# A two-layer hybrid attention backbone: SBUF-only elementwise work of the attention phases moved from VectorE and ScalarE to GpSimd

## Chip, cores and metric

The kernel runs on one core of one Trainium2 chip, in one launch. The metric is the device time in microseconds. The engines are called by their short names: PE (TensorE), DVE (VectorE), ACT (ScalarE), POOL (GpSimd) and SP (SyncE, which here only issues DMAs).

## What is computed

Two layers of a flow-matching backbone work on 512 latent tokens and 256 context tokens of width 1024, in fp32. Each layer, cut to what matters:

```python
hx = rms_norm(x, p['norm1_g']) * (1 + sc1x) + sh1x      # adaLN modulation from SiLU(c); ctx likewise
(lw_q, ..., ln_v) = split_in(hx @ p['w_in'])            # one projection to 3072 columns
out_w = window_attention(q, k, v, k_c, v_c, p['a_sink'])           # group A: windowed, rotary, sink
out_f = rms_norm(diff_attention(q, k, v, k_c, v_c, lam)) * ...     # group B: P0 - lam * P1, rotary
out_r = rms_norm(o_f + flip(o_b), p['c_gn_g']) * gate              # group C: retention, no softmax
out_n = neighbourhood_attention(q, k, v, k_c, v_c, p['d_rpb'])     # group D: 2-D neighbourhood, bias
x = x + g1x * (concat(out_w, out_f, out_r, out_n) @ p['w_out'])
x = x + g2x * (square(relu(h2 @ p['w_mlp1'])) @ p['w_mlp2'])
```

The context stream goes the same way in the first layer; the output is the latent stream.

## The kernel before

**Precision by halves.** Every large product is made of three matmuls. An fp32 value is split into a rounded part `hi` (type fp32r) and a remainder `lo = src - hi`; the product is hi\*hi + hi\*lo + lo\*hi. `split` (L274 to L276) does this: ACT copies `src` to `hi` with rounding (L275), DVE subtracts (L276).

```python
def split(src, hi, lo):
    S.activation(hi, src, AF.Copy)
    V.tensor_tensor(lo, src, hi.bitcast(F32), op=OP.subtract)
```

It is used for weights (`wload`, L278: tiles `wh` and `wl`, 128x512, four buffers of each), for transposed probabilities (`pth`, `ptl`, from PSUM), for C's decayed scores (L963 to L965: `P` is in SBUF, again `pth` and `ptl`), for B's stacked queries and keys (`sp`, in `stack32`, L617) and for the attention outputs ahead of the output projection (`oh`, `ol`, in `out_ac`, L1033). `kstack` (L603) does the same by hand for the keys of A, C and D (`ks`, `kl`, L610), 64 partitions at a time, and SP copies each part to the other 64 partitions.

**Stages.** A layer has an attention phase and an MLP phase. In the attention phase seven units stand in the order a0 b0 b1 c0 c1 d0 d1. Each has an input part (`in_a` to `in_d`: input projection, norms, rotary embedding, stacking) and an attention part (`at_a` to `at_d`: scores, probabilities, transposition, product with V). `weave` (L106) runs a unit's attention part and fills in the input parts of later units and then the output projection (`out_ac`), by planned costs and leads, so that PE has gemm work between the steps of an attention chain. The framework's scheduler then turns the program into one fixed order of instructions per engine, with priorities: a weight's split gets a bonus of 40 (`WPRI`). Each engine works off its own order and stops at an instruction whose input isn't there.

**The chains in the attention parts.** A and D (`band_pair`, L726) take two score tiles at a time: row maximum on DVE, exponential with row sum on ACT (L752), reciprocal on DVE, normalisation of each tile on ACT (L759), transposition on PE. B (`at_b`, L832) needs no normalisation of that kind: DVE combines two exponentials (L860). C multiplies scores by a decay table on DVE (L962), splits the result and goes straight to the product with V, where `pvmm` (L699) issues matmuls with `pth` (L703) and `ptl` (L702, L705). The decay tables `tb` and `tx` of a head come from `ctables` (L895): loads, exponentials, and two sums of 128x512 on DVE (L915). The rotary embedding (L651 to L656): ACT scales, DVE shuffles, multiplies by the cosine table (L654), multiplies the shuffled copy by the sine table, adds.

`PTS` = 5 buffers are shared by `pth`, `ptl` and the copies of outputs; `htile` tiles (16) hold first the normalised input of the phase and then, buffer by buffer as the last input tile no longer needs them, `oh` and `ol`.

## Time and profile before

| | us |
|---|---|
| median of 3 runs | 1896.78 (1894.79 to 1897.86) |
| profiled execution, its own time | 1897.64 |
| span of the profile | 1895.6 |
| PE busy in the span | 1843.1 (97%) |
| DVE busy | 1307.4 (69%) |
| ACT busy | 973.4 (51%) |
| POOL busy | 0.2 (4 instructions) |

The span is what the hardware profiler recorded on the core; the execution's own time has 2.0 us around it. Attention of layer 0 lies at about 100 to 520 us, the MLP of layer 0 to about 1120, attention of layer 1 at 1130 to 1560, its MLP after that. A busy PE isn't PE at its peak: matmuls overlap, and a matmul's recorded length is longer than its distance to the next. The chain that ended last, followed back from the end, lies on PE for 89% of the span.

### The profile page before, as it was taken

To read this page: it belongs to the slowest core of one execution; us is meant where nothing else is said; L and a number is where in the kernel's file an instruction comes from. 1 tells how busy PE (TensorE), PEld (TensorE's weight loads), DVE (VectorE), ACT (ScalarE), POOL (GpSimd) and SP (SyncE) were. 2 spreads that over 40 slices of the span, in tenths; PEclk is the share of its full clock that TensorE was granted. 3 is DMA by queue.
4 is the path that set the end of the run, shared out by engine and by line. 5 is a ranking of instruction groups with operands and counts; after the bars stand their busy time and mean duration, and the time that the engine had idled before them with its cause. 6 is when DMAs were issued, how large, how long until landed. Compare 5 with 4: busy or idle time off the path is not lost.

```text
span 1895.6 us, 29665 instructions
## 1 busy us (share of the span) xinstructions
PE 1843.1 (97%) x10899; PEld 1519.8 (80%) x10899; DVE 1307.4 (69%) x3005; ACT 973.4 (51%) x1934; POOL 0.2 (0%) x4
## 2 busy tenths in 40 slices
PE   7998889999999999999999999999899999999999
PEld 3786667778878888888888777878677788989897
DVE  5788867788777847847847367898788764545453
ACT  4677656668654214223323356877577763334242
POOL 0000000000000000000000000000000000000000
PEclk8999989999999999999999999999899999999999
DMA  8324334432323523423422352332243223232322
GB/s 297 99 79 122 100 120 131 148 95 65 109 95 106 157 93 117 151 95 117 150 95 89 111 172 83 83 96 79 85 133 95 75 95 100 90 100 90 100 90 95
DMA packets 110417, 208.68 MB, mean 110 GB/s; under 512 B 14272, under 2 KB 20160, under 8 KB 110272
## 3 DMA queue, kind: packets, MB, share of 16 engines
q1 hardware_dynamic: 110272, 206.78, 34.7%
q8 instruction: 86, 1.41, 0.3%
q14 instruction: 59, 0.48, 0.1%
HBM read 182.09 MB, written 5.24 MB: 99 GB/s over the span
## 4 chain that ended last, share of the span: by engine, by line
PE 89%; ACT 5%; DVE 3%; DMA 2%; issue 1%; SPq 0%; ACTq 0%; DVEq 0%
PE mm L315 23%; PE mm L317 23%; PE mm L316 23%; PE ps L697 3%; PE po L703 2%; PE po L705 2%; PE ps L262 1%; PE ps L850 1%; PE pt L241 1%; ACT pth L275 1%; PE pt L257 1%; PE pt L869 1%; PE pt L798 1%; ACT P L856 1%; DMA zm<-in_dd_dram 1%
## 5 line engine op out<-in xcount | busy, mean ns | idle before, releaser
L275 ACT ACTIVATE wh<-wr 128x512 fp32r<-128x512 f32 (+1 forms) x414 | 252.9, 614 | 645.3 <-PE mm L316 605.0
L317 PE MATMUL mm<-hh,wl 128*128 128x512 f32 (+2 forms) x1680 | 548.8, 327 | 6.7 <-DVE wl L276 6.6
L315 PE MATMUL mm<-hh,wh 128*128 128x512 f32 (+2 forms) x1680 | 551.2, 328 | 3.0 <-ACT zq L651 1.7
L316 PE MATMUL mm<-hl,wh 128*128 128x512 f32 (+2 forms) x1680 | 549.8, 327 | 0.0
L276 DVE TENSOR_TENSOR wl<-wr,wh 128x512 fp32r<-128x512 f32 (+1 forms) x414 | 275.4, 667 | 162.4 <-ACT wh L275 156.4
L315 PEld LDWEIGHTS mm<-hh,wh 128*128 128x128 f32 x1680 | 318.3, 190 | 39.9 <-issue 7.6
L317 PEld LDWEIGHTS mm<-hh,wl 128*128 128x128 f32 x1680 | 318.9, 190 | 34.7 <-DVE wl L276 7.7
L316 PEld LDWEIGHTS mm<-hl,wh 128*128 128x128 f32 x1680 | 318.0, 189 | 28.1 <-issue 3.5
L316 PE MATMUL mm<-ml,wh 128*128 128x512 f32 (+1 forms) x768 | 273.2, 356 | 0.0
L315 PE MATMUL mm<-mh,wh 128*128 128x512 f32 (+1 forms) x768 | 272.7, 356 | 0.0
L317 PE MATMUL mm<-mh,wl 128*128 128x512 f32 (+1 forms) x768 | 272.4, 355 | 0.0
L316 PEld LDWEIGHTS mm<-ml,wh 128*128 128x128 f32 x768 | 145.2, 189 | 24.5 <-issue 4.5
L315 PEld LDWEIGHTS mm<-mh,wh 128*128 128x128 f32 x768 | 145.2, 189 | 21.9 <-issue 0.4
L317 PEld LDWEIGHTS mm<-mh,wl 128*128 128x128 f32 x768 | 145.1, 189 | 21.2 <-issue 1.2
L394 DVE SCALAR_TENSOR_TENSOR acc<-wm,silp,acc 128x512 f32<-128x512 f32 x196 | 138.9, 747 | 21.9 <-DMA wm<-in_wmod_dram 21.7
L1127 DVE SCALAR_TENSOR_TENSOR x<-mm,modc,x 128x512 f32<-128x512 f32 (+1 forms) x96 | 63.4, 660 | 116.6 <-PE mm L317 116.6
L703 PE MATMUL po<-pth,vv 128*128 128x256 f32 (+2 forms) x328 | 105.5, 328 | 8.9 <-ACT pth L275 8.1
L276 DVE TENSOR_TENSOR ptl<-pt,pth 128x512 fp32r<-128x512 f32 (+3 forms) x148 | 92.4, 630 | 27.9 <-ACT pth L275 26.4
L275 ACT ACTIVATE pth<-pt 128x512 fp32r<-128x512 f32 (+3 forms) x148 | 80.2, 547 | 32.2 <-PE pt L869 21.6
L1111 DVE TENSOR_TENSOR zq<-mm,nacc 128x256 f32<-128x256 f32 (+1 forms) x128 | 61.9, 484 | 44.5 <-PE mm L317 43.0
L703 PEld LDWEIGHTS po<-pth,vv 128*128 128x128 f32 x328 | 61.8, 189 | 32.3 <-ACT pth L275 24.0
L705 PE MATMUL po<-ptl,vv 128*64 128x256 f32 (+2 forms) x256 | 78.3, 318 | 2.9 <-DVE ptl L276 2.3
(251 smaller groups left out, 2701.3 us busy)
## 6 DMA issues: line engine op xcount, KB each, us to landing
wr<-in_w_dram SPq DMA_DIRECT2D x272, 256.0 KB, 2.6
wm<-in_wmod_dram SPq DMA_DIRECT2D x112, 256.0 KB, 2.8
wr<-in_win_dram SPq DMA_DIRECT2D x96, 256.0 KB, 3.0
wr<-in_wmodh_dram SPq DMA_DIRECT2D x48, 256.0 KB, 3.3
st<-sp SPq DMA_DIRECT2D x96, 96.0 KB, 2.2
w<-in_wmod_dram SPq DMA_DIRECT2D x16, 384.0 KB, 7.1
tx<-in_dd_dram SPq DMA_DIRECT2D x8, 512.0 KB, 4.4
zm<-in_dd_dram SPq DMA_DIRECT2D x16, 256.0 KB, 3.5
```

What stands on the lines that cost most here:

```text
L241: T.matmul(pj, lhsT=gmean[w], rhs=sq[:, 256 * j:256 * j + 256], start=True, stop=add is None)
L275: S.activation(hi, src, AF.Copy)
L276: V.tensor_tensor(lo, src, hi.bitcast(F32), op=OP.subtract)
L315: T.matmul(p, lhsT=wh, rhs=ah[:, s:s + l], start=(k == 0), stop=False)
L316: T.matmul(p, lhsT=wh, rhs=al[:, s:s + l], start=False, stop=False)
L317: T.matmul(p, lhsT=wl, rhs=ah[:, s:s + l], start=False, stop=(k == len(act) - 1))
L394: V.scalar_tensor_tensor(acc[:, v], r, sil[:, k, v:v + 1], acc[:, v], op0=OP.mult, op1=OP.add)
L697: T.matmul(o, lhsT=x, rhs=y, start=(i == 0), stop=(i == 1))
L703: T.matmul(po[:, c0:c0 + l], lhsT=vv[:, hh, t], rhs=ph, start=start, stop=stop)
L705: T.matmul(po[0:64, c0:c0 + l], lhsT=vv[:, hh, t, 0:64], rhs=pl, start=False, stop=False)
L1111: V.tensor_tensor(r[:, s:s + l], p[:, :l], y2[:, s:s + l], op=OP.mult)
L1127: V.scalar_tensor_tensor(xx, p, modc[:, 40 + m, s // 512:s // 512 + 1], xx, op0=OP.mult, op1=OP.add)
```

## The change

In the attention phases these operations go from DVE to POOL, unchanged in shape and operands: the remainders of weights (128 instructions), of C's scores (56), of the keys of A, C and D (20), of B's stacked queries and keys (8), and of the attention outputs of groups A, B and C (12), the product with the cosine table in the rotary embedding (14), and the sums of C's decay tables (16). The normalisation of the probabilities of A and D (80) goes from ACT to POOL, as a product with a per-row scalar. The remainders of transposed probabilities stay on DVE, since these read PSUM, and in the MLP phases (`wrest[0] = V` behind the attention phase) the weights' remainders stay there too. Priorities, buffers and `weave`'s costs are the same. Behind the first two added lines, numbers of lines in the changed kernel are 2 to 4 higher (L915 becomes L918, L705 L708).

```diff
--- before.py
+++ after.py
@@ -154,7 +154,7 @@
 @with_exitstack
 def body(ctx: ExitStack, tc, A):
     nc = tc.nc
-    V, S, G, T, SY = nc.vector, nc.scalar, nc.gpsimd, nc.tensor, nc.sync
+    V, S, PL, T, SY = nc.vector, nc.scalar, nc.gpsimd, nc.tensor, nc.sync
 
     cons = ctx.enter_context(tc.tile_pool(name="cons", bufs=1))
     main = ctx.enter_context(tc.tile_pool(name="main", bufs=1))
@@ -271,9 +271,11 @@
             V.scalar_tensor_tensor(sq[:, s:s + l], ap, EPS if eps else 0.0, sq[:, s:s + l], op0=OP.add, op1=OP.mult)
         V.scalar_tensor_tensor(sq[:, :n], sq[:, :n], -3.0, e3[:, :n], op0=OP.add, op1=OP.mult)
 
-    def split(src, hi, lo):
+    def split(src, hi, lo, eng=V):
         S.activation(hi, src, AF.Copy)
-        V.tensor_tensor(lo, src, hi.bitcast(F32), op=OP.subtract)
+        eng.tensor_tensor(lo, src, hi.bitcast(F32), op=OP.subtract)
+
+    wrest = [PL]
 
     def wload(src, k0=0, k1=8, dst=None):
 
@@ -288,7 +290,7 @@
                 hi = wp.tile([128, 512], F32R, name=nm("wh"), tag="wh", bufs=WB)
                 lo = wp.tile([128, 512], F32R, name=nm("wl"), tag="wl", bufs=WB)
             with tc.high_priority(offset=WPRI):
-                split(r, hi[:, :128 * n], lo[:, :128 * n])
+                split(r, hi[:, :128 * n], lo[:, :128 * n], wrest[0])
             res += [(hi[:, 128 * k:128 * k + 128], lo[:, 128 * k:128 * k + 128]) for k in range(n)]
         return res
 
@@ -467,6 +469,7 @@
         rb = rowb[:, L, :]
         modc = modcs[L]
 
+        wrest[0] = PL
 
         att = ExitStack()
         ap_ = att.enter_context(tc.tile_pool(name=f"att{L}", bufs=1))
@@ -607,7 +610,7 @@
                 a, b = HALF[h], HALF[1 - h]
                 S.activation(x[a, :n], t[a, :n], AF.Copy)
                 KCOPY(x[b, :n], x[a, :n])
-                V.tensor_tensor(y[a, :n], t[a, :n], x[a, :n].bitcast(F32), op=OP.subtract)
+                PL.tensor_tensor(y[a, :n], t[a, :n], x[a, :n].bitcast(F32), op=OP.subtract)
                 KCOPY(y[b, :n], y[a, :n])
             return st, lo
 
@@ -617,7 +620,7 @@
         def stack32(t, n, order):
 
             parts = [main.tile([128, 768], F32R, name=nm("sp"), tag="zq", bufs=ZQ)[:, :n] for _ in range(2)]
-            split(t[:, :n], *parts)
+            split(t[:, :n], *parts, PL)
             st = [u3r("st") for _ in range(4)]
             for i, x in enumerate(st):
                 for r, w in enumerate(order):
@@ -651,7 +654,7 @@
                     S.activation(t[:, 0:512], p, AF.Copy, scale=gc)
                     sh = zq()
                     V.stream_shuffle(sh[:, 0:512], t[:, 0:512], mask)
-                    V.tensor_tensor(t[:, 0:512], t[:, 0:512], tab[:, 0], op=OP.mult)
+                    PL.tensor_tensor(t[:, 0:512], t[:, 0:512], tab[:, 0], op=OP.mult)
                     V.tensor_tensor(sh[:, 0:512], sh[:, 0:512], tab[:, 1], op=OP.mult)
                     V.tensor_tensor(t[:, 0:512], t[:, 0:512], sh[:, 0:512], op=OP.add)
                 elif permute and s == 0:
@@ -756,7 +759,7 @@
                 V.tensor_tensor(sm[:, 6:8], sm[:, 6:8], sm[:, 10:12], op=OP.add)
             V.reciprocal(sm[:, 12:14], sm[:, 6:8])
             for i, (P, _, w) in enumerate(res):
-                S.activation(P[:, :w + 256], P[:, :w + 256], AF.Copy, scale=sm[:, 12 + i:13 + i])
+                PL.tensor_scalar(P[:, :w + 256], P[:, :w + 256], sm[:, 12 + i:13 + i], None, op0=OP.mult)
             yield 0
             return [(P, kts) for P, kts, _ in res]
 
@@ -912,7 +915,7 @@
                 SY.dma_start(out=tw[:, 0:512], in_=A['dd'][:, 1920 + 512 * t:2432 + 512 * t])
                 S.activation(tw[:, 0:512], tw[:, 0:512], AF.Exp, scale=nlb)
                 S.activation(tx[:, t], tx[:, t], AF.Exp, scale=lf)
-                V.tensor_tensor(tx[:, t], tx[:, t], tw[:, 0:512], op=OP.add)
+                PL.tensor_tensor(tx[:, t], tx[:, t], tw[:, 0:512], op=OP.add)
             return tb, tx
 
         def in_c(u):
@@ -961,7 +964,7 @@
                         P = ptile()
                         V.tensor_tensor(P[:, :l], p[:, :l], dk, op=OP.mult)
                         pth, ptl = ptt()
-                        split(P[:, :l], pth[:, :l], ptl[:, :l])
+                        split(P[:, :l], pth[:, :l], ptl[:, :l], PL)
                         pvmm(po, 0, l, vv, hh, t, pth[:, :l], ptl[:, :l], i == 0, i == len(kts) - 1)
                         yield 3 * l * .43
                     ev = evac_t(po, l)
@@ -1035,7 +1038,7 @@
             osp = []
             for c in range(6):
                 hi, lo = htile("oh"), htile("ol")
-                split(of[c][:, :nq], hi[:, :nq], lo[:, :nq])
+                split(of[c][:, :nq], hi[:, :nq], lo[:, :nq], PL)
                 osp.append((hi, lo))
             for m in range(8):
                 xr = u3("xr")
@@ -1055,6 +1058,7 @@
         cost_at = {x: c * 1e3 for x, c in zip('abcd', [[CA0, CB0, CC0, CD0], [CA1, CB1, CC1, CD1]][L])}
         weave(units, ins, ats, cost_in, cost_at, out_ac(), [[L0_0, L0_1, L0_2, L0_3, L0_4, L0_5, L0_6, L0_7], [L1_0, L1_1, L1_2, L1_3, L1_4, L1_5, L1_6, L1_7]][L], lambda: tc.high_priority(offset=BOOST))
         att.close()
+        wrest[0] = V
 
 
         mlp = ExitStack()
```

The scheduler orders all engines anew. Three places:

The first is on DVE before, in layer 1, at the end of c0's input part (`zq`, `gt` are C's gate, `zm` and `gp` its tables, `sm` and `P` belong to B); `wl` is the remainder of a weight tile.

```order
L933 SCALAR_TENSOR_TENSOR zq_14184<-zq_14184,zq_14187 128x512
L903 TENSOR_SCALAR zm_14198<-gp_14194,lg_11949 128x128
L934 SCALAR_TENSOR_TENSOR gt_14183<-gt_14183,gsc_11929,zq_14184 128x512
L904 TENSOR_SCALAR gp_14194<-gp_14194,nlg_11983 128x128
L276 TENSOR_TENSOR wl_14427<-wr_14424,wh_14426 128x512
L905 TENSOR_TENSOR gp_14194<-gp_14194,zm_14198 128x128
L724 ISA P_14292,sm_14291<-ps_14294,zcol 128x256
```

In the changed kernel the same tile stands on POOL behind other weight tiles:

```order
L276 TENSOR_TENSOR wl_14233<-wr_14230,wh_14232 128x512
L276 TENSOR_TENSOR wl_14239<-wr_14236,wh_14238 128x512
L276 TENSOR_TENSOR wl_14421<-wr_14418,wh_14420 128x512
L276 TENSOR_TENSOR wl_14427<-wr_14424,wh_14426 128x512
L918 TENSOR_TENSOR tx_14195<-tx_14195,zm_14206 128x512
L918 TENSOR_TENSOR tx_14195<-tx_14195,zm_14211 128x512
```

`wl_14427` no longer stands behind the gate and the tables; behind it on POOL come the two sums of a table.

The second is C in layer 0, first head, six score tiles of 512 columns. On DVE before, from the second tile's remainder (`P` is the decayed score, `tx` the next head's table):

```order
L276 TENSOR_TENSOR ptl_3797<-P_3794,pth_3796 128x512
L962 TENSOR_TENSOR P_3915<-ps_3906,gp_3383 128x512
L276 TENSOR_TENSOR ptl_3836<-P_3833,pth_3835 128x512
L962 TENSOR_TENSOR P_3938<-ps_3929,gp_3383 128x512
L276 TENSOR_TENSOR ptl_3895<-P_3892,pth_3894 128x512
L915 TENSOR_TENSOR tx_3734<-tx_3734,zm_3745 128x512
L915 TENSOR_TENSOR tx_3734<-tx_3734,zm_3750 128x512
L276 TENSOR_TENSOR ptl_3918<-P_3915,pth_3917 128x512
L336 TENSOR_TENSOR modc_124<-mm_3849,colc 128x4
L962 TENSOR_TENSOR P_4016<-ps_3962,gp_3383 128x256
L276 TENSOR_TENSOR ptl_3941<-P_3938,pth_3940 128x512
```

On POOL in the changed kernel, from the first tile's remainder:

```order
L276 TENSOR_TENSOR ptl_3774<-P_3771,pth_3773 128x512
L276 TENSOR_TENSOR ptl_3797<-P_3794,pth_3796 128x512
L276 TENSOR_TENSOR wl_4005<-wr_4002,wh_4004 128x512
L276 TENSOR_TENSOR ptl_3836<-P_3833,pth_3835 128x512
L276 TENSOR_TENSOR ptl_3895<-P_3892,pth_3894 128x512
L918 TENSOR_TENSOR tx_3734<-tx_3734,zm_3745 128x512
L918 TENSOR_TENSOR tx_3734<-tx_3734,zm_3750 128x512
L276 TENSOR_TENSOR ptl_3918<-P_3915,pth_3917 128x512
L276 TENSOR_TENSOR ptl_3941<-P_3938,pth_3940 128x512
```

The products `P` stay on DVE; the six remainders now share POOL's order with a weight's remainder and with the two sums of the next head's table.

The third is PE at the same place, from the third tile's remainder as weights of a matmul (`ptl_3836`) to the fifth tile. Before:

```order
L705 MATMUL po_3755<-ptl_3836,vv_2936 64x512
L703 MATMUL po_3755<-pth_3894,vv_2936 128x512
L316 MATMUL mm_4008<-hl_224,wh_3998 128x512
L697 MATMUL ps_4024<-qs_3161,ks_2711 128x256
L697 MATMUL ps_4024<-qs_3161,kl_2713 128x256
L317 MATMUL mm_4008<-hh_223,wl_3999 128x512
L315 MATMUL mm_4008<-hh_225,wh_4004 128x512
L705 MATMUL po_3755<-ptl_3895,vv_2936 64x512
L316 MATMUL mm_4008<-hl_226,wh_4004 128x512
L317 MATMUL mm_4008<-hh_225,wl_4005 128x512
L703 MATMUL po_3755<-pth_3917,vv_2936 128x512
```

In the changed kernel:

```order
L708 MATMUL po_3755<-ptl_3836,vv_2936 64x512
L706 MATMUL po_3755<-pth_3894,vv_2936 128x512
L319 MATMUL mm_3876<-hh_223,wl_3866 128x256
L317 MATMUL mm_3876<-hh_225,wh_3871 128x256
L708 MATMUL po_3755<-ptl_3895,vv_2936 64x512
L318 MATMUL mm_3876<-hl_226,wh_3871 128x256
L319 MATMUL mm_3876<-hh_225,wl_3872 128x256
L317 MATMUL mm_3876<-hh_227,wh_3871 128x256
L318 MATMUL mm_3876<-hl_228,wh_3871 128x256
L319 MATMUL mm_3876<-hh_227,wl_3872 128x256
L317 MATMUL mm_3876<-hh_229,wh_3871 128x256
L318 MATMUL mm_3876<-hl_230,wh_3871 128x256
```

The gemm matmuls between the consumers of `ptl` were of 512 columns and belonged to a later tile; now they have 256 columns, and `ptl_3836` and `ptl_3895` are consumed four rows apart.

## Rows read from the trace of the kernel before

**Rows 1.** The page, part 1: busy time of each engine (share of the span), instructions.
```profile
PE 1843.1 (97%) x10899; PEld 1519.8 (80%) x10899; DVE 1307.4 (69%) x3005; ACT 973.4 (51%) x1934; POOL 0.2 (0%) x4
```

**Rows 2.** Windows: start:end, length, busy us (instructions) of each engine, clock, DMA.
```profile
100.00:520.00 420.00, 398.08 (x2495) 317.39 (x2494) 330.08 (x908) 291.68 (x639) 0.00 (x0) 0.98 0.36 108
600.00:1100.00 500.00, 500.00 (x2801) 426.90 (x2800) 321.63 (x550) 153.42 (x249) 0.00 (x0) 1.00 0.36 116
1130.00:1560.00 430.00, 415.74 (x2349) 328.40 (x2348) 343.81 (x868) 302.50 (x625) 0.00 (x0) 0.99 0.32 95
```

**Rows 3.** Waits of PE over the span: who, for whom, us, times, longest.
```profile
PE po L703 <- ACT pth L275: 8.1, 15, 1.0
PE mm L317 <- DVE wl L276: 6.6, 2, 3.4
PE pt L869 <- DVE P L860: 3.3, 5, 0.8
```

**Rows 4.** Timeline, layer 1, 1324 to 1352: start, us, engine, line, operation, wait before.
```profile
1324.14 0.63 ACT L275 ACTIVATE wh<-wr 128x512 fp32r<-128x512 f32 x1
...
1334.47 0.67 DVE L276 TENSOR_TENSOR wl<-wr,wh 128x512 fp32r<-128x512 f32 x1
1335.19 0.79 PE L317 MATMUL mm<-hh,wl 128*128 128x512 f32 x1 [3.17 <-DVE wl L276]
1335.79 0.63 PE L315 MATMUL mm<-hh,wh 128*128 128x512 f32 x1
1336.21 0.63 PE L316 MATMUL mm<-hl,wh 128*128 128x512 f32 x1
...
1351.14 0.80 PE L317 MATMUL mm<-hh,wl 128*128 128x512 f32 x1 [3.39 <-DVE wl L276]
```

**Rows 5.** Windows around the two stalls of rows 4 (columns as in rows 2).
```profile
1318.00:1350.00 32.00, 24.30 (x131) 18.74 (x129) 28.70 (x78) 22.46 (x45) 0.00 (x0) 0.89 0.16 44
1335.20:1340.20 5.00, 5.00 (x12) 3.94 (x13) 4.85 (x14) 3.10 (x7) 0.00 (x0) 0.50 0.60 175
1351.20:1354.20 3.00, 3.00 (x7) 2.43 (x8) 3.00 (x7) 0.32 (x3) 0.00 (x0) 0.51 0.80 230
```

**Rows 6.** Groups by line: form, count, busy us, mean ns, idle before and releaser.
```profile
L275 ACT ACTIVATE wh<-wr 128x512 fp32r<-128x512 f32 (+1 forms) x414 | 252.9, 614 | 645.3 <-PE mm L316 605.0 <-issue 27.2 <-DMA wr<-in_win_dram 9.6
L276 DVE TENSOR_TENSOR wl<-wr,wh 128x512 fp32r<-128x512 f32 (+1 forms) x414 | 275.4, 667 | 162.4 <-ACT wh L275 156.4 <-issue 1.3 <-PE po L703 0.2
L610 DVE TENSOR_TENSOR kl<-zq,ks 64x768 fp32r<-64x768 f32 x20 | 19.0, 949 | 1.3 <-ACT ks L608 0.9
L276 DVE TENSOR_TENSOR ol<-of,oh 128x768 fp32r<-128x768 f32 (+1 forms) x16 | 13.0, 818 | 1.5 <-ACT oh L275 1.5
L759 ACT ACTIVATE P<-P,sm 128x512 f32<-128x512 f32 (+2 forms) x80 | 55.1, 715 | 4.8 <-DVE sm L757 3.8 <-DVE sm L853 1.0
```

**Rows 7.** Timeline of PE in C, layer 0: starts of neighbouring matmuls at full clock.
```profile
342.38 0.39 PE L697 MATMUL ps<-qs,ks 128*128 128x512 f32 x1
342.61 0.39 PE L697 MATMUL ps<-qs,kl 128*128 128x512 f32 x1
...
345.53 0.28 PE L697 MATMUL ps<-qs,ks 128*128 128x256 f32 x1
345.64 0.28 PE L697 MATMUL ps<-qs,kl 128*128 128x256 f32 x1
345.76 0.39 PE L317 MATMUL mm<-hh,wl 128*128 128x512 f32 x1
```

**Rows 8.** Timeline of DVE, same head: first and last of its six 512-column remainders.
```profile
342.73 0.68 DVE L276 TENSOR_TENSOR ptl<-P,pth 128x512 fp32r<-128x512 f32 x1
...
350.53 0.68 DVE L276 TENSOR_TENSOR ptl<-P,pth 128x512 fp32r<-128x512 f32 x1
```

**Rows 9.** Groups of DVE with two inputs in SBUF that stay on DVE.
```profile
L860 DVE SCALAR_TENSOR_TENSOR P<-P,sm,P 128x768 f32<-128x768 f32 (+1 forms) x40 | 36.1, 904 | 0.3
L600 DVE TENSOR_TENSOR qs<-zq,qs 64x768 fp32r<-64x768 f32 (+1 forms) x24 | 19.7, 819 | 2.0 <-ACT qs L599 1.2
```

## Prediction

> **What bounds the kernel now.** I read the engine totals first: TensorE (PE) is busy 1843.1 of 1895.6 us, VectorE (DVE) 1307.4, ScalarE (ACT) 973.4, and GpSimd (POOL) has four instructions in all [rows 1]. Then the same by stage: in an MLP stretch PE is busy for all of 500 us; in the two attention phases it is idle for 420.0 - 398.1 = 21.9 us and 430.0 - 415.7 = 14.3 us [rows 2]. So the change, which touches the attention phases alone, can win back some 36 us of visible idleness and what the clock loses beside it, and no more. DVE (79% and 80%) and ACT (69% and 70%) are the engines that PE waits for there.
>
> The waits say how: over the span PE waited 8.1 us for the rounded halves of transposed probabilities from ACT, 6.6 us in two stalls for a weight remainder from DVE, and 3.3 us for B's probabilities from DVE [rows 3]. The two long stalls stand in the timeline [rows 4]: ACT's rounding of a weight starts at 1324.14 and takes 0.63 us, but DVE comes to a remainder (`wl`) only at 1334.47, behind other work in its fixed order, and a matmul starts at 1335.19 after 3.17 us of nothing; the same again at 1351.14, 3.39 us. Behind each the granted clock is at half (0.50 and 0.51), the 1.2 GHz level, for 12 and 7 matmuls [rows 5]. In this stretch DVE is busy 28.7 of 32.0 us.
>
> **What the change removes: gains.** (a) The two stalls cost 6.6 us, and the half clock 12 x 0.2 + 7 x 0.2 = 3.8 us more (0.42 us from one 512-column matmul to the next [rows 4], where the full clock, 2.4 GHz, has 0.23 [rows 7]): 10.4 us. On POOL `wl_14427` follows weight remainders and no attention work, so these stalls should go. DVE's backlog there stays the next thing late: one `wl` and two `tx` of about 0.67 us and two `kl` of 0.95 leave it, 3.9 us of the 28.7. I take 7 us, between 3.9 and 10.4. (b) ACT gives up 80 normalisations of 0.715 us (55 us of its 291.7 + 302.5), DVE the remainders. Of the 8.1 + 3.3 us of waits for them I take 5; bounds 0 and 11.4.
>
> **The price on POOL.** No row shows an elementwise instruction on POOL. Bounds from the nearest rows, for 128x512 with two inputs: DVE's own 0.667 us, and two passes of ACT's one-input copy, 2 x 0.614 = 1.23 us [rows 6]. Below DVE's price I see no reason to go. I take 1.23, by ACT's row: an engine that has to fetch both operands one after the other is the dear case, and an error there costs more than it saves. For the single-input normalisation the bounds are 0.715 and 2 x 0.715 = 1.43 us; I take the middle, 1.07. The upper bound of all is each instruction held behind one DVE instruction as well, 1.23 + 0.667 = 1.9 us.
>
> The Trainium skill (GPSIMD Engine Reference, section 3.1, Elementwise — side-by-side cycle accounting) gives a two-input add of 2048 fp32 as 1.96 times DVE's time; the estimate by that page would be 0.667 x 1.96 = 1.31 us, and the sum below would end some 4 us higher. No run here shows it yet.
>
> **What the change adds: losses.** (c) C's score remainders (56 `ptl`) sit on the path to C's second matmul, and here the new order has become tight. In layer 0's first head DVE now starts the first of six at 342.73 and the last at 350.53, 7.8 us later [rows 8], and the PE order has input-projection work of 512 columns between their consumers. In the changed order only 13 matmuls of 512 columns, 22 of 256 and a few tiny ones stand between those two consumers: 13 x 0.23 + 22 x 0.115 + 0.3 = 5.8 us [rows 7]. POOL has eight two-input instructions to do in that time (five `ptl`, one `wl`, two `tx`): 8 x 1.23 = 9.8 us, so PE stands 4.0 us. The same count for the other tight stretches: layer 0, second head, 5 x 1.23 - 5.2 = 0.9; third head, 8 x 1.23 + 2 x 0.62 - 9.0 = 2.1 (0.62 for half the columns); layer 1, first head, 13 x 1.23 - 15.2 = 0.8; second head, with two `kl` at 0.949 x 1.23 / 0.667 = 1.75 [rows 6], 8 x 1.23 + 2 x 1.75 - 11.2 = 2.1. Together 10. At DVE's price every one of them is below zero, so the term is 0; at 1.9 us (and `kl` and half forms in proportion) it is 9.4 + 4.3 + 8.1 + 9.5 + 9.4 = 41.
>
> (d) The 12 `ol` at the start of the output projection: layer 0 wants five of 768 columns (0.667 to 1.23 as above, so 1.85 each) and two `wl` within 6.7 us of PE work: 5 x 1.85 + 1.23 + 0.62 = 11.1, 4.4 late, of which the last input tile's 24 matmuls of 256 columns, during which the buffers come free one by one, hide 24 x 0.115 = 2.8. That leaves 2; layer 1 is covered by more such matmuls. Bounds 0 and 5. (DVE's mean of 0.818 [rows 6] mixes 768 and 512 columns.)
>
> (e) Normalisation of A and D. Counted in the order, the median of PE work from a D pair's last score to its first transposition falls from 8.0 to 5.5 us, with five of 20 pairs at 4.9 or less; A's falls from 8.9 to 7.6. A pair is two instructions in a row, so POOL delivers the second 2 x (1.07 - 0.715) = 0.7 us later than ACT would. For A the remaining distance hides it. For D I take those five pairs, 5 x 0.7 = 3.5 us; bounds 0 and 20 x 0.7 = 14.
>
> (f) New stalls drop the clock as the old ones did. Two of them, at the price of the two seen: 3.8 us; bounds 0 and twice that.
>
> At nothing I cost these. The 128 weight remainders: their buffers come free about 10 us of PE work ahead of their first use, and a load, rounding and 1.23 us fit in; if that cover went, PE would wait as at 1335. The `kl` and `sp` copies: SP issues the copies between partitions behind them and has weight loads queued after these, so each load can start up to 0.9 us later, inside the same 10 us. The 14 rotary products: POOL's 1.23 us runs beside DVE's shuffle and second product. The 16 table sums beyond those counted in (c): prepared a head ahead.
>
> **Sum.** -7 - 5 + 10 + 2 + 3.5 + 3.8 = +7.3 us on the profiled execution's 1897.64 (its span and 2.0 us around it), which is 1904.9; the median of the three runs is 0.9 lower, so 1904.0. A measurement of this kernel tells about 0.2%, 3.8 us, from no change; this is 0.4%.
>
> **Rivals.**
> 1. Faster: POOL is quick enough. In (c) the point from which it decides is 5.8 / 8 = 0.73 us for an instruction; DVE's 0.667 is under it. Then (c) to (f) are nothing and both gains come in full or nearly: 1896.8 - 10.4 - 5 = 1881. For it: DVE's row; the order leaves wide room for weights. Against: an engine that matches DVE on two inputs would be the best case I can bound.
> 2. No change: the losses are met by the gains, 12 against 12, 1897, as would come out at about 1.1 us an instruction.
> 3. Much slower: POOL and DVE hold each other up. DVE keeps 40 sums of B's probabilities (0.904 us), 24 query remainders (0.819) and more with both inputs in SBUF [rows 9]; if a POOL instruction waits behind one each time, its price is 1.9 us, and (c), (d), (e), (f) become 41 + 5 + 10 + 7.6 = 64 against 12 of gains: +52, 1949. Half of that, 1923, if only every second one waits. Against: most of DVE's work in C reads PSUM.
>
> The Trainium skill (SBUF — State Buffer, Who interferes with whom) says that a DVE instruction with two SBUF inputs and a GpSimd instruction that reads SBUF exclude each other for their whole length. That is rival 3's mechanism; no row here shows it, as POOL did nothing before.
>
> That the change does not do what it says I leave out: the order shows the instructions on POOL.
>
> **Chances and range.** Slower by over 0.2%: my forecast, 0.42, and rival 3, 0.13, together 0.55. Rival 1, 0.30; rival 2, 0.15. The likeliest case's own range is 1901 to 1918. For 8 in 10 I go down to rival 1's 1881 less 1 and up to 1932, between the half and the whole of rival 3.
>
> **What would show it.** Right: POOL busy some 350 to 450 us, its 128x512 remainders spaced at 1.1 to 1.3 us; PE waiting on POOL `ptl` in the C stages and on POOL `P` in D, more than 10 us together; no 3 us wait for `wl` near 1335 and 1351. Wrong: remainders under 0.73 us, or PE waits on POOL under 5 us, or DVE's two-input instructions clearly longer than 0.904 and 0.819, which would be rival 3.

## The result and the profile after

The changed kernel takes 2026.22 us (median of 4 runs, 2024.55 to 2027.56) where the kernel before takes 1897.32: ratio 1.0681, 95% interval [1.0662, 1.0699], 129 us slower. The forecast was 1904 with a range up to 1932, so the sign was right and the size far off.

The page of the changed kernel, part 1, against [rows 1], and its granted clock (the kernel before had a span of 1895.6 us at 0.990):

```profile
PE 1890.4 (93%) x10899; PEld 1532.8 (76%) x10899; DVE 1234.7 (61%) x2751; ACT 930.5 (46%) x1854; POOL 469.3 (23%) x338
core 0: 2025.7 us, clock 0.978
```

DVE lost 73 us of busy time, ACT 43, and POOL has 469. DVE should have lost far more: the 254 instructions that left it took 176 us in the kernel before, added up by form, and those that stay take some 75 us longer than they did (records overlap, so the busy time does not fall by exactly the difference). Of the 130 us that the span grew, 2025.7 - 1890.4 - (1895.6 - 1843.1) = 83 us are idle PE and 47 us the same 10899 matmuls taking longer. If the mean clock is a mix of its two levels, (1 - 0.978) / 0.5 x 2025.7 = 89 us ran at half clock instead of 38, and half of the 51 more, some 26 us, are lost by it. What makes the other 20 us of longer matmul records no run tells.

Where the idleness is, by windows of the changed kernel (columns as in [rows 2]; attention of layer 0, MLP, attention of layer 1, which lie later here):

```profile
100.00:600.00 500.00, 435.69 (x2552) 332.90 (x2551) 304.17 (x818) 271.55 (x600) 220.52 (x162) 0.96 0.31 92
700.00:1200.00 500.00, 499.89 (x2823) 425.39 (x2821) 322.98 (x552) 158.51 (x262) 0.00 (x0) 1.00 0.36 119
1215.00:1690.00 475.00, 428.78 (x2312) 330.62 (x2312) 304.05 (x740) 279.72 (x585) 218.98 (x151) 0.96 0.27 82
```

PE is idle for 64.3 and 46.2 us in the two attention phases, and the MLP is as full as before. DVE and ACT, which PE used to wait for, are at 61 to 64% and 54 to 59%: less loaded, and yet the phase is slower. The waits of PE over the span name the new partner (compare [rows 3]):

```profile
PE pt L801 <- POOL P L762: 28.6, 23, 2.5
PE pt L1016 <- POOL P L762: 22.1, 22, 2.2
PE po L708 <- POOL ptl L276: 21.9, 27, 2.0
...
PE pt L872 <- DVE P L863: 4.1, 8, 1.2
PE mm L318 <- POOL ol L276: 3.6, 4, 1.2
...
PE po L705 <- POOL ptl L276: 2.8, 3, 1.6
...
PE po L706 <- ACT pth L275: 1.6, 3, 0.9
```

`P` of A (L801) and D (L1016) is what the normalisation writes, `ptl` is C's remainder (L705 and L708), `ol` the outputs'. The 6.6 us of weight stalls and most of the 8.1 us for ACT's `pth` are gone; the 3.3 us for B's probabilities are 4.1. What an instruction costs on POOL (groups by form: count, busy us, mean ns, idle before):

```profile
L276 POOL TENSOR_TENSOR wl<-wr,wh 128x512 fp32r<-128x512 f32 x110 | 149.4, 1362 | 920.5 <-ACT wh L275 868.1 <-PE mm L318 16.9 <-PE mm L319 8.4
L276 POOL TENSOR_TENSOR ptl<-P,pth 128x512 fp32r<-128x512 f32 x48 | 63.8, 1342 | 35.2 <-ACT pth L275 28.5 <-PE mm L319 4.1 <-PE ps L700 2.5
L762 POOL TENSOR_SCALAR P<-P,sm 128x640 f32<-128x640 f32 x32 | 60.3, 1893 | 34.2 <-DVE sm L760 29.3 <-issue 4.9
L762 POOL TENSOR_SCALAR P<-P,sm 128x512 f32<-128x512 f32 x32 | 50.0, 1567 | 33.4 <-DVE sm L760 15.2 <-DVE sm L753 12.4 <-ACT P L859 5.6
L762 POOL TENSOR_SCALAR P<-P,sm 128x256 f32<-128x256 f32 x16 | 14.6, 927 | 16.4 <-DVE sm L760 11.9 <-PE mm L344 3.0 <-PE mm L318 1.5
```

The two-input remainder is near the price taken (1.34 to 1.36 us against 1.23). The normalisation is not: 1.57 us at 512 columns and 1.89 at 640, 1.57 on average, dearer than the two-input form, where 1.07 was taken and 1.43 was the bound. One pair of A in the timeline shows what that does:

```profile
130.13 3.75 POOL L762 TENSOR_SCALAR P<-P,sm 128x640 f32<-128x640 f32 x2 [4.91 <-issue]
132.06 0.20 PEld L801 LDWEIGHTS pt<-ident,P 128*128 128x128 f32 x2 [1.24 <-POOL P L762]
132.07 0.44 PE L801 MATMUL pt<-ident,P 128*128 128x128 f32 x2 [0.92 <-POOL P L762]
133.93 0.64 PEld L801 LDWEIGHTS pt<-ident,P 128*128 128x128 f32 x6 [1.50 <-POOL P L762]
```

PE stops twice for one pair: for the first tile, which POOL has after 1.9 us, and again for the second.

And something that the waits don't name. DVE's groups, in the changed kernel (in the kernel before: L863, there L860 in [rows 9], 1011 ns at 768 columns alone; L753, there L750, 162; `ptl<-pt` 688):

```profile
L276 DVE TENSOR_TENSOR ptl<-pt,pth 128x512 fp32r<-128x512 f32 x116 | 78.6, 688 | 61.2 <-ACT pth L275 60.4
L863 DVE SCALAR_TENSOR_TENSOR P<-P,sm,P 128x768 f32<-128x768 f32 x32 | 36.1, 1127 | 0.4
L753 DVE TENSOR_SCALAR sm<-sm 128x2 f32<-128x2 f32 x40 | 12.3, 308 | 0.4
```

DVE's instructions that read PSUM (`pt`) are as long as before; those with all operands in SBUF that are shown here are longer, a two-column one on average twice as long. (Not every one is: the softmax's reciprocal takes 162 ns, before 161.) In all forms together B's sums take 1046 ns on average instead of 904, and the query remainders 1027 instead of 819: the sign that the prediction named for rival 3.

### The profile page after: what moved, and what is told of

Its sections match the earlier page's. It is cut to its first block, busy times and chain, and to the rows that moved or that the text cites. A ratio compares the mean times of both kernels' runs of the same rounds, so it can differ in the third digit from the quotient of the medians.

```text
span 2025.7 us, 30057 instructions
## 1 busy us (share of the span) xinstructions
PE 1890.4 (93%) x10899; PEld 1532.8 (76%) x10899; DVE 1234.7 (61%) x2751; ACT 930.5 (46%) x1854; POOL 469.3 (23%) x338
## 5 line engine op out<-in xcount | busy, mean ns | idle before, releaser
L276 POOL TENSOR_TENSOR wl<-wr,wh 128x512 fp32r<-128x512 f32 x126 | 162.2, 1293 | 927.9 <-ACT wh L275 875.4
L276 DVE TENSOR_TENSOR wl<-wr,wh 128x512 fp32r<-128x512 f32 (+1 forms) x288 | 194.0, 674 | 143.6 <-ACT wh L275 139.9
L319 PEld LDWEIGHTS mm<-mh,wl 128*128 128x128 f32 x768 | 145.1, 189 | 21.2 <-issue 1.2
L762 POOL TENSOR_SCALAR P<-P,sm 128x512 f32<-128x512 f32 (+2 forms) x80 | 124.5, 1569 | 84.0 <-DVE sm L760 56.5
L708 PE MATMUL po<-ptl,vv 128*64 128x256 f32 (+2 forms) x256 | 80.6, 328 | 22.2 <-POOL ptl L276 21.9
```

Source lines behind the costliest of these rows:

```text
L276: eng.tensor_tensor(lo, src, hi.bitcast(F32), op=OP.subtract)
L319: T.matmul(p, lhsT=wl, rhs=ah[:, s:s + l], start=False, stop=(k == len(act) - 1))
L708: T.matmul(po[0:64, c0:c0 + l], lhsT=vv[:, hh, t, 0:64], rhs=pl, start=False, stop=False)
L762: PL.tensor_scalar(P[:, :w + 256], P[:, :w + 256], sm[:, 12 + i:13 + i], None, op0=OP.mult)
```

## The experiments

Two theories were set against each other. **Path**: POOL is slower, and where PE waits for its result the difference is paid. **Exclusion** (rival 3): POOL and DVE hold each other up at SBUF, whoever waits for the result. Lines are those of the changed kernel.

### One part of the change at a time

Each kernel is the kernel before with one part of the change. e1, the normalisations; e2, C's remainders; e3, the weights (`wrest[0]` is POOL in the attention phases); e4, all the rest (the changed kernel's other lines, not shown here):

```diff
e1
-                S.activation(P[:, :w + 256], P[:, :w + 256], AF.Copy, scale=sm[:, 12 + i:13 + i])
+                PL.tensor_scalar(P[:, :w + 256], P[:, :w + 256], sm[:, 12 + i:13 + i], None, op0=OP.mult)
e2
-                        split(P[:, :l], pth[:, :l], ptl[:, :l])
+                        split(P[:, :l], pth[:, :l], ptl[:, :l], PL)
e3
-                split(r, hi[:, :128 * n], lo[:, :128 * n])
+                split(r, hi[:, :128 * n], lo[:, :128 * n], wrest[0])
```

> The kernel before with the 80 normalisations of A and D alone on POOL. Theory 1 (path: what costs is that POOL is slower where PE waits for its result; in the changed kernel PE waited 28.6 + 22.1 us for POOL's P, of 76.8 us of waits on POOL in all, and the whole rise was 129 us): about 129 x 50.7 / 76.8 = +85 us, 1982. Theory 2 (exclusion: every POOL instruction holds DVE's SBUF-only instructions up, so the cost goes with POOL's busy time; these are 126 of its 469 us): +34 us, 1931.

> The kernel before with C's 56 score remainders alone on POOL. Theory 1 (path; PE waited 21.9 us of 76.8 for POOL's ptl): about +37 us, 1934. Theory 2 (exclusion by busy time, 70 of 469 us): +19 us, 1916.

> The kernel before with the 128 weight remainders of the attention phases alone on POOL. Theory 1 (path; PE waited 0.6 us for POOL's wl, and the 6.6 us of waits for DVE's wl are gone): 0 to -10 us, 1887 to 1897. Theory 2 (exclusion by busy time; the weights are the largest part, 166 of 469 us): +45 us, 1942.

> The kernel before with the remaining parts alone on POOL: remainders of keys and of stacked queries, the first rotary product, C's table sums, the outputs' remainders. Theory 1 (path; PE waited 3.6 us for POOL's ol): 0 to +6 us, 1897 to 1903. Theory 2 (exclusion by busy time, 107 of 469 us): +29 us, 1926.

| on POOL | us | ratio, interval | over before |
|---|---|---|---|
| e1 normalisations | 1951.95 | 1.0292 [1.0271, 1.0314] | +53 |
| e2 C's remainders | 1921.96 | 1.0126 [1.0111, 1.0141] | +23 |
| e3 weights | 1909.58 | 1.0061 [1.0046, 1.0076] | +11 |
| e4 the rest | 1913.36 | 1.0084 [1.0065, 1.0103] | +14 |

Each of the four lies between its two forecasts, so neither theory has any of them by itself. By POOL's time the weights (166 us) should cost most and cost least; by path they and the rest should cost little or nothing and don't. In e3 DVE's busy time fell only from 1307.4 to 1294.0 us, though 84 us of work had left it. The parts make 101 of the 129 us.

### Exclusion by itself

e5 leaves every weight remainder on DVE and adds a POOL instruction beside it whose result nobody reads; e6 does the same with 2 columns. The order of the other engines is unchanged in both. (`scr` is the scratch tile and `att_on[0]` is true in the attention phases; the lines that set them are not shown.)

```diff
-                split(r, hi[:, :128 * n], lo[:, :128 * n])
+                split(r, hi[:, :128 * n], lo[:, :128 * n], wrest[0]); att_on[0] and PL.tensor_tensor(scr[:, :128 * n], hi[:, :128 * n].bitcast(F32), hi[:, :128 * n].bitcast(F32), op=OP.subtract)
```

> The kernel before, with DVE still making every weight remainder, and POOL in addition subtracting each rounded weight from itself into a scratch tile that nobody reads (128 instructions in the attention phases, of the size of the remainders). The order of all other engines is word for word that of the kernel before, and no engine waits for these results. Exclusion (a POOL instruction and a DVE instruction that keeps to SBUF hold each other up): slower, by the 11 us of the run with the weights on POOL or more, since DVE is not relieved here: 1908 to 1917 us; DVE's SBUF-only instructions some 50 us longer in sum. Path or order alone: 1897 to 1899 us, DVE's instructions unchanged.

> The control for the run before it: the same 128 added POOL instructions at the same places with the same waits, but of 2 columns each. All theories: as the kernel before, 1897 to 1899 us. If it is slower too, waits and issue of the added instructions cost, and not the time that they hold SBUF.

e5: 1924.24 us, 1.0138 [1.0120, 1.0156], +27 us, more than was expected. e6: 1900.33, 1.0006 [0.9993, 1.0019], no difference. So 156 us of POOL reading SBUF cost 27 us with no path, no new order and no relief lost; the waits and the issue of the added instructions cost nothing that shows. DVE, with the same instructions in the same order, is busy 1353.6 us in e5 and 1307.8 in e6. The timeline shows it at one place. First e5, then the same instruction in e6:

```profile
146.19 0.69 DVE L276 TENSOR_TENSOR ptl<-pt,pth 128x512 fp32r<-128x512 f32 x1
...
146.66 1.04 POOL L293 TENSOR_TENSOR scr<-wh 128x512 f32<-128x512 f32 x1 [11.52 <-ACT wh L275]
...
146.80 0.92 DVE L759 TENSOR_TENSOR sm<-sm 128x2 f32<-128x2 f32 x1
```

```profile
146.79 0.15 DVE L759 TENSOR_TENSOR sm<-sm 128x2 f32<-128x2 f32 x1
```

A sum of two columns, 0.15 us long, takes 0.92 and ends at 147.72, when POOL's instruction ends (147.70). It stands in the chain of a softmax, and everything behind it on DVE waits too. The group of DVE's second rotary product (two inputs in SBUF) and a group that reads PSUM, e5 and then e6:

```profile
L276 DVE TENSOR_TENSOR ptl<-pt,pth 128x512 fp32r<-128x512 f32 x116 | 79.0, 686 | 23.8 <-ACT pth L275 23.1
L658 DVE TENSOR_TENSOR zq<-zq,rt 128x512 f32<-128x512 f32 x14 | 13.2, 940 | 0.0
```

```profile
L276 DVE TENSOR_TENSOR ptl<-pt,pth 128x512 fp32r<-128x512 f32 x116 | 79.3, 688 | 26.7 <-ACT pth L275 25.7
L658 DVE TENSOR_TENSOR zq<-zq,rt 128x512 f32<-128x512 f32 x14 | 9.6, 685 | 0.0
```

The Trainium skill (SBUF — State Buffer, Who interferes with whom) states this exclusion for DVE instructions with two SBUF inputs and for one-input ones in a two-port mode. The rows agree for two inputs (L658) and for the PSUM readers, which it leaves out. L753, with one input, was longer too (above), but no row shows in which mode it ran.

### The normalisations: path

e11 leaves the normalisation on ACT and adds a POOL scaling of a scratch tile of the same size by the same reciprocal; e12 with 2 columns. Both also have 14 buffers instead of 8 for `sm`, the tile with a pair's maxima, sums and reciprocals, so e12 and not the kernel before is the control. The line of e11 below stands behind the normalisation, which stays. e9 really moves the first tile of each pair and leaves the second on ACT.

```diff
e11
+; PL.tensor_scalar(scr[:, :w + 256], scr[:, :w + 256], sm[:, 12 + i:13 + i], None, op0=OP.mult)
e9
+                PL.tensor_scalar(P[:, :w + 256], P[:, :w + 256], sm[:, 12:13], None, op0=OP.mult) if i == 0 else S.activation(P[:, :w + 256], P[:, :w + 256], AF.Copy, scale=sm[:, 13:14])
```

> The kernel before, with ACT still normalising, and POOL in addition scaling a scratch tile of the same size by the same reciprocal (80 instructions); nobody waits for it. Against its control (the next run, whose order on the other engines is word for word this one's). Exclusion at the rate of the first dummy run, 26.6 us for 166 us of POOL: 126 x 0.16 = +20 us. Path (in the run with the normalisations on POOL, PE's waits for P were 45 us and DVE's instructions only 11 us longer): +8 us at most.

> The control: the same 80 added instructions, of 2 columns each. The order of the other engines differs a little from that of the kernel before (some 1750 lines of difference on PE), so it also shows what such a change of order costs by itself. Path and exclusion: 1895 to 1901 us. Order: clearly off 1897 in either direction.

> The kernel before with the first normalisation of each A and D pair on POOL and the second on ACT, so that the two run side by side. In the run with all 80 on POOL a pair of 640 columns took 3.75 us there, where ACT takes 1.54. Now it is ready after 1.89 us at the latest, 0.35 later than on ACT (512 columns: 1.57 against 1.43, 0.14). Path: of 53 us at most 40 x 0.3 = 12 are left, 1898 to 1910 us. Exclusion, in proportion to POOL's time: half of 53, 1925 us.

e11: 1898.91 us, 1.0000 [0.9988, 1.0013]; e12: 1899.70, 0.9999 [0.9986, 1.0012]. Here exclusion costs nothing, though POOL works 131 us, and the somewhat different order of the same work doesn't either. DVE is held less here: it is busy 1313.6 us against 1309.0 in e12. So the 53 us of e1 are not exclusion. What is left is the path, on which PE waits 25.0 + 19.6 us for POOL's `P` in e1; the order of e1, which is further from the kernel before than that of e12, no run tries by itself. How tight the path was before shows in one pair of D in the kernel before:

```profile
439.36 1.44 ACT L759 ACTIVATE P<-P,sm 128x512 f32<-128x512 f32 x2 [0.63 <-DVE sm L757]
...
440.27 0.38 PE L1013 MATMUL pt<-ident,P 128*128 128x128 f32 x2
...
440.96 0.82 PE L1013 MATMUL pt<-ident,P 128*128 128x128 f32 x6
```

ACT has the pair at 440.80, and PE goes on at 440.96 behind the first two transpositions. Over all 40 pairs the first transposition started only 0.5 us (median) after the first tile was normalised. In e1 the second tile comes some 2 us later than from ACT, and of PE's waits for `P` 28 us are for second tiles (26 waits) and 16 for first ones (17 waits).

e9: 1910.5 us, 1.0061 [1.0041, 1.0082], +11, near the most that the path theory gave, though PE does not wait where that had it. PE's waits in e9:

```profile
PE pt L801 <- POOL P L762: 11.1, 12, 1.6
PE pt L1016 <- POOL P L762: 10.1, 11, 1.6
```

21.2 us in 23 waits, 0.92 each, where the pair is ready at most 0.35 us later. One of them in the timeline:

```profile
134.83 1.88 POOL L762 TENSOR_SCALAR P<-P,sm 128x640 f32<-128x640 f32 x1 [8.70 <-DVE sm L757]
135.09 0.81 ACT L762 ACTIVATE P<-P,sm 128x640 f32<-128x640 f32 x1
...
136.77 0.44 PE L801 MATMUL pt<-ident,P 128*128 128x128 f32 x2 [0.83 <-POOL P L762]
```

PE transposes the first tile first. From ACT that tile came after 0.8 us, from POOL after 1.9, and PE stops for it. The second tile is there by then, and the whole cost is 11 us, half of these waits and near the 12 expected from the 0.35 us by which the pair is late. The other 42 of the 53 us come only when the second tile stands behind the first on POOL.

### In company

The changed kernel with one part taken back: e7, the normalisations on ACT; e10, the weights on DVE (each the - line of e1 and e3 in place of the + line).

> The changed kernel with the normalisations back on ACT. Parts that add up: 2026 - 54 (what the normalisations alone cost) = 1972 us. Queueing (the normalisations also stood behind weights and rotary products on POOL's one queue, and these behind them; the four parts alone add up to 101 of 129 us): the whole missing 28 us comes back as well, 1944 to 1955 us.

> The changed kernel with the weight remainders back on DVE. Additive parts: 2026 - 11 (what the weights alone cost) = 2015 us. Queueing (the normalisations cost 80 us in the changed kernel and 53 alone; if they stand behind weight remainders on POOL's queue, the 27 between come back with the weights): 1988 us, and a share of it where other parts of the queue hold them up as well.

e7: 1946.48 us, 1.0253 [1.0231, 1.0275]: 80 us come back, not 53, and what is left, 49 us, is the sum of the other three parts (48). So the missing 28 us belong to the normalisations in company. e10: 2005.94, 1.0568 [1.0540, 1.0597]: 20 us come back, not 11 and not 38. Company with the weights, be it on POOL's queue, by exclusion or by the order, is then a third of it. The lag behind the kernel before, from the first and last transposition of each stage, shows where (us lost in the stage; a minus is a gain; C has no transpositions of probabilities, so its stage is what lies between B's last and D's first):

| | start | A 0 | B 0 | C 0 | D 0 | to layer 1 | A 1 | B 1 | C 1 | D 1 |
|---|---|---|---|---|---|---|---|---|---|---|
| changed | 7.0 | 18.8 | 2.4 | 24.5 | 21.2 | 10.9 | 18.1 | -6.0 | 15.2 | 14.2 |
| e1 | -0.2 | 14.0 | -1.8 | -1.1 | 13.4 | 3.7 | 12.9 | 1.9 | -2.9 | 12.2 |
| e7 | 5.9 | 2.7 | -1.1 | 22.4 | 0.3 | 9.6 | 2.4 | -3.2 | 7.7 | 5.6 |
| e5 | 5.1 | 2.7 | 5.1 | 0.0 | 3.2 | 3.0 | 1.0 | 3.1 | 1.0 | 2.0 |

A and D are the normalisations' (e1), C is not (e7). What the other two thirds are (C's remainders and the outputs on the queue, exclusion, the new order) no run tells apart.

### C's remainders: both

In e2 PE's waits for POOL's remainder are short and many, and POOL was mostly not behind with its work (the waits of PE, and those of POOL itself):

```profile
PE po L708 <- POOL ptl L276: 12.9, 23, 1.0
PE po L705 <- POOL ptl L276: 3.8, 7, 0.8
POOL ptl L276 <- ACT pth L275: 1372.6, 34, 945.0
```

POOL stood idle before 34 of its 56 remainders until ACT's `pth` came (the 1372.6 us hold all the time outside C). So PE mostly waits for a remainder that started in time and takes 0.7 us more than on DVE (1.40 against 0.68 us on average), not for a line of POOL instructions.

e14 leaves C's remainders on DVE and adds a POOL instruction beside each that nobody reads (behind the line of `split`, which stays).

```diff
+; PL.tensor_tensor(scr[:, :l], pth[:, :l].bitcast(F32), pth[:, :l].bitcast(F32), op=OP.subtract)
```

> The kernel before, with DVE still making C's 56 score remainders, and POOL in addition subtracting each rounded score tile from itself into a scratch tile that nobody reads; order of the other engines as before but for 4 lines of PE. Exclusion at the first dummy run's rate: 70 x 0.16 = +11 us, 1908 (of the 23 us that the move itself cost). Path (in the run with these on POOL, PE waited 17 us for them): the dummy costs nothing, 1897 to 1900 us.

1912.91 us, 1.0075 [1.0061, 1.0088], +13. DVE's own remainders are held, 926 ns instead of 683, and PE's wait for them grows from 2.3 to 9.3 us:

```profile
L276 DVE TENSOR_TENSOR ptl<-P,pth 128x512 fp32r<-128x512 f32 x48 | 44.4, 926 | 0.9 <-issue 0.7
```

So exclusion weighs in C. How much of e2's 23 us it is can't be read from this, since in e2 DVE has no such remainders to be held; there PE waited 16.7 us for POOL's, and DVE's other instructions were some 18 us longer in sum.

### The gain (a), and the parts costed at nothing

e8 puts only layer 1's weights on POOL, e13 only the 16 of C's input projection there (the line that ends this behind C's input part is not shown); e15 rotary products and table sums, e16 keys and stacked queries, e18 the outputs' remainders.

```diff
e8
+        wrest[0] = PL if L else V
e13
+            wrest[0] = PL if L else V; k = yield from cqk(kstack, f'ck{u}', NT, 1.0)
e15
+                    PL.tensor_tensor(t[:, 0:512], t[:, 0:512], tab[:, 0], op=OP.mult)
+                PL.tensor_tensor(tx[:, t], tx[:, t], tw[:, 0:512], op=OP.add)
e16
+                PL.tensor_tensor(y[a, :n], t[a, :n], x[a, :n].bitcast(F32), op=OP.subtract)
+            split(t[:, :n], *parts, PL)
e18
+                split(of[c][:, :nq], hi[:, :nq], lo[:, :nq], PL)
```

> The kernel before with the weight remainders of layer 1's attention phase alone on POOL; layer 0 is word for word as before. In the run with both layers' weights on POOL layer 0 lost 16.6 us up to layer 1's first transposition and layer 1 won 5.5 from there on. If the two stalls of the kernel before are what is won: 1891 to 1894 us. If exclusion costs as much in layer 1: 1897 us or more.

> The kernel before with only the 16 weight remainders of C's input projection in layer 1 on POOL; among them are the two for which PE stalled 3.2 and 3.4 us. Gain (a) of the prediction (two stalls and the half clock behind them, 3.9 to 10.4 us; 16 x 1.3 us of POOL at the dummy run's rate of 0.16 would cost 3.4): 1888 to 1894 us. If the stalls are only handed on to the next late thing: 1897 us or more.

> The kernel before with the 14 first rotary products and the 16 table sums alone on POOL (both costed at nothing in the prediction; the rotary products ran at 1.73 to 1.80 us beside DVE's second product instead of 1.28). Exclusion at 0.16 of their 44 us: +7 us, 1904. Path alone: 1897 to 1899.

> The kernel before with the 20 key and 8 stacked-query remainders alone on POOL (costed at nothing). Exclusion at 0.16 of their 52 us: +8 us, 1905. Path alone: 1897 to 1899.

> The kernel before with the 12 remainders of the outputs alone on POOL. The remaining parts together cost 14 us, while two of their three pairs, alone, win 6.6 and 5.2. If the parts add up, the outputs cost 26 us: 1924. If it is their company that costs (exclusion among more POOL work and DVE work in the same stretch, and a new order): what PE waited for POOL's ol, 1.5 to 3.6 us, and no more: 1897 to 1902 us.

| on POOL | us | ratio, interval |
|---|---|---|
| e8 weights of layer 1 | 1897.77 | 1.0004 [0.9994, 1.0015] |
| e13 16 of them, C's | 1891.96 | 0.9963 [0.9949, 0.9977] |
| e15 rotary, tables | 1892.82 | 0.9967 [0.9955, 0.9979] |
| e16 keys, queries | 1894.22 | 0.9973 [0.9964, 0.9983] |
| e18 outputs | 1903.32 | 1.0030 [1.0018, 1.0042] |

The gain (a) exists: 7.5 us in e13, with few weights beside the two that had stalled. PE's waits for `wl` are gone there, and the stretch of [rows 5] from 1318 to 1350, where PE was busy 24.3 us at a granted clock of 0.89, reads in e13 (1.00 is the full clock):

```profile
1318.00:1350.00 32.00, 29.24 (x172) 23.95 (x171) 28.43 (x76) 24.55 (x48) 5.36 (x4) 1.00 0.21 61
```

With all of layer 1's weights the gain is given back (e8). Exclusion at e5's rate failed as a forecast for e15 and e16: they should have cost 7 and 8 us and win 7 and 5. Whether they win by what DVE no longer does or by the new order no run tells. e18 ends a little above the second of its two expectations. The three pairs of e4 add up to -7 - 5 + 6 = -6 us and cost 14 together, so 20 us of e4 come only in company again.

### A version that beats both

e17 joins rotary products and tables in layer 0 with e13's weights in layer 1: the lines of e15 with `(V if L else PL)`, and e13's.

> The kernel before with the first rotary product and the table sums on POOL in layer 0 alone and the 16 weight remainders of C's input projection on POOL in layer 1 alone. Its order is word for word that of the run with rotary products and tables in layer 0 (which led by 5.4 to 7.8 us when layer 0 was done) and that of the run with C's weights in layer 1 (which won 5.6 us there). If each stage's gain stands by itself: 11 to 13 us off, 1885 to 1888 us. If one gives back what the other won: 1891 to 1893 us.

1885.41 us (5 runs, 1882.30 to 1887.36), 0.9933 [0.9919, 0.9946], 12 us faster than the kernel before: the two gains stand side by side, with 31 instructions moved instead of 334.

## Why the prediction was wrong

- **Where PE would wait**: right. The waits for POOL's `ptl` in C and `P` in D are there, the two stalls are gone, POOL's 469 us are just above the 350 to 450 named. That A has the longest wait of all was not foreseen.
- **The price on POOL**: 1.23 us for two inputs was right in size; the estimate by the Trainium skill (GPSIMD Engine Reference, section 3.1), 1.31, is nearer to the 1.34 measured. The one-input price failed: 1.57 on average against 1.07. The step "I take the middle" took its bounds from ACT's rows, and POOL lies above the upper one, 1.43: its one-input product is 0.2 us dearer than its two-input remainder at 256 and at 512 columns.
- **Term (e) failed, and is the largest part of the miss**: +3.5 (0 to 14) against 53 us alone and 80 in company. It failed at two sentences. "POOL delivers the second 2 x (1.07 - 0.715) = 0.7 us later": with the measured price it is 3.75 - 1.54 = 2.2 us (on ACT a 640-column pair of the kernel before took 1.54), and the first tile is 1.1 us late (e9). "For A the remaining distance hides it", and for D only five pairs: A lost 14 and 13 us, D 13 and 12 (e1). The distance, 8.0 and 8.9 us before and 5.5 and 7.6 in the changed order, was counted in PE work from the last score, but the chain of maximum, exponential, reciprocal and normalisation had used it up: in the kernel before 0.5 us (median) were left between the first tile and its first transposition.
- **Term (c)**: 10 (0 to 41) against 23. That PE waits there held, the count did not: it priced a line of up to thirteen instructions on POOL, and e2 loses 23 us with the remainders alone on POOL, most of which stood in no line. What is paid is each remainder's own lateness, and exclusion on top (e14) in a share that stays open.
- **Term (d)**: 2 (0 to 5) against 6 (e18), of which PE's waits for POOL's `ol` show 1.7. **Term (f)**: 3.8 against some 26 by the mean clock, as there were not two new stalls but some 80 waits for POOL.
- **Gain (a)**: 7 against 7.5 (e13), the best of the terms; but the other weights cost it and more (e3, e8). **Gain (b)**: 5 against 6.5 less of waits for ACT's `pth` and 0.8 more for B's probabilities; no run shows it apart.
- **At nothing, the weights**: 11 alone and 20 in company. The argument, buffers free 10 us ahead, was right for the path: PE doesn't wait for POOL's `wl`. It left out what POOL does to DVE meanwhile (e5), which the prediction has in rival 3 but does not price for the weights. Keys, queries, rotary products and tables at nothing: alone they win 12 us.
- **Rival 3** had 0.13 and the right mechanism, with the wrong victim: it priced POOL held behind DVE, 1.9 us an instruction, where POOL's remainders of weights took 1.29 us in the median and 1.36 on average. It is DVE that is held, some 75 us in sum, and a 0.15 us instruction for 0.92. Even the whole of rival 3, 1949, lies far below the 2026 measured. What was said against it, that most of DVE's work in C reads PSUM, is true of the rows and didn't save C (e14).
- **The sum** added parts as if alone. 28 of the 129 us come only when the normalisations meet the other parts. One queue, exclusion and the new order are all possible there; 9 of the 28 go with the weights (e10), and the rest stays open.

## What to carry to other kernels

Price an operation that is moved to a slower engine tile by tile, as the consumer takes its results, against the time that is left between a result and its use, and not at the average distance between instructions. Before GpSimd gets SBUF work, list what VectorE keeps with its operands all in SBUF, the shortest instructions above all: each can be held for a whole GpSimd instruction, and a dummy instruction that nobody reads measures that apart from everything else. Move a few operations at a time, where a wait is to be won, and not a class of them.

## What was not expected of the hardware

A two-column VectorE instruction (0.15 us) ended only with the GpSimd instruction beside it (0.92 us), and no wait shows this: the time lies inside the instruction's length. A GpSimd multiplication by a per-row scalar took longer than a subtraction of two tiles: 1.57 against 1.34 us for 128x512, 0.93 against 0.73 for 128x256. And the price of exclusion differs by place: 156 us of GpSimd beside the weights cost 27 us and made VectorE 46 us busier (e5), 131 us behind the softmax's reciprocals cost nothing and made it 5 us busier (e11). The first reads two tiles and the second one, so whether the neighbours or the form of the instruction decide was not tested apart.
